# Seven-product blocks with product copies ahead of weight operations, four direct blocks for five, and attention scores on 128 rows

## The chip, the cores and the metric

The kernel runs on one core of one Trainium2 chip. TensorE (PE) multiplies, VectorE (DVE), ScalarE (ACT) and GpSimd (POOL) work on the operands, and SyncE (SP) issues nearly all transfers. The metric is the device time of one execution in microseconds (us), as the median of several runs of the same kernel.

## What is computed

Two layers, each a feed-forward network (FFN), a token mixer and a second FFN, on 512 tokens of width 1024, all in float32. The feed-forward width is 2816, or 22 blocks of 128 columns.

```python
def swiglu(h, w_in, w_out):
    gu = h @ w_in
    g, u = jnp.split(gu, 2, axis=-1)
    return (jax.nn.silu(g) * u) @ w_out

def reference(x, norm_gain, ...):
    for layer in range(DEPTH):                      # 2
        g = norm_gain[layer]
        h = swiglu(rms_norm(x, g[0]), ffn_w_in[layer, 0], ffn_w_out[layer, 0])
        x = x + 0.5 * rms_norm(h, g[1])
        h = token_mixer(rms_norm(x, g[2]), ...)
        x = x + rms_norm(h, g[3])
        h = swiglu(rms_norm(x, g[4]), ffn_w_in[layer, 1], ffn_w_out[layer, 1])
        x = x + 0.5 * rms_norm(h, g[5])
    return x
```

The mixer projects its input once and runs two groups of heads on the result: 8 attention heads of width 64 with a windowed mask, and 4 mLSTM heads of width 128 in both directions. Both groups go through one output projection.

## The kernel before

**Products.** Every float32 operand is split into two halves, `hi` (a cast on ACT) and `lo` (the difference, on DVE), and a product is the sum of three matmuls: hi by hi, hi by lo, lo by hi (lines 246 to 248 in the FFN's first product). One product of the kind used there is 4 such triples, 12 matmuls of 256 columns.

**The FFN's first product** (`ffn_in`) goes over the 22 blocks f of 128 columns of gate and up weights. The first `ne` = 5 blocks are *direct* (`block`): for each half of the tokens, the gate and the up weights are loaded, split, and multiplied in 4 products, 8 products or 96 matmuls for a whole block. The other 17 go through a Strassen-Winograd scheme (`seven`): 7 products, 84 matmuls, from sums of the weight quarters (`ws`, made on DVE at lines 311 to 314), the raw gate weights, the last quarter of the up weights (`a22`) and sums of the token quarters (`tq`, `xf`, made once at the start of the FFN). A block `seven(f, w, nxt)` also prepares the weights of the block after it, `nxt`: `nxt.sums`, `nxt.raw`, `nxt.one`, `nxt.two` and `nxt.last` each start with a cast on ACT (line 288) and go on with a difference on DVE (line 290). Between them stand the block's own evacuations of products: ACT copies `ha` and `hb` (lines 341, 352, 356), DVE sums `ht`, `hc`, `hb` (343, 362, 366). Inside `tc.manual_schedule` PE, DVE and ACT run in the order in which the code is written, so that an evacuation written behind a weight operation waits for it. Everywhere else a scheduler orders the work by its place in the program and by when buffers come free.

**Slots.** Large buffers are slots with one tile each at a time. `xf`, two tiles with sums of token quarters, lies in slots 17 and 19. At the end of the direct blocks `xx.finish()` splits `xf[0]` into `xh` and `xl` (ACT line 219, DVE line 220); after that slot 17 is free. `Weights(f)` loads the gate weights into a ring of three buffers, `raw`, and the up weights into `wu`, slot 17 + 2·(f mod 2). For f = `ne` + 1 the up weights go into the ring instead. With `ne` = 5 the first `Weights` uses slot 19.

**The mixer.** `proj_nat` projects for 128 or 256 tokens at a time. For the first four column groups the second weight half's `lo` is made on POOL (`sub=G`), while DVE still works on the norm of the sublayer's input (`post`, `pre`). `mixer_gates` makes the gates' rows with a chain of small DVE operations. `stack_pair(hp)` turns the keys and queries of a pair of attention heads: `kst` and `qsh` have 128 rows, hi and lo halves of 64 rows on top of each other, and `qsl` holds the lo half of the queries in 64 rows of one head each. `scores(n)` makes a tile of scores by two matmuls of 512 columns, `qsh` by `kst` on 128 rows (line 854) and `qsl` by `kst` on 64 rows (line 855), 64 times in the two layers. The mLSTM heads run beside the projections of the attention's operands, the attention beside the output projection, both paced in a fixed ratio.

**The start.** `pre(t, ...)` norms token tile t: two squares on ACT, a root, two products `nt` on DVE (line 178), and eight transposes on PE (line 182).

Of the kernel before, what the change touches and what calls it, by code (L numbers as in the profile page):

```python
# [41 lines left out]
def trunk_kernel(ctx, tc, x, norm_gain, ffn_w_in, ffn_w_out, mix_w_in, conv_w, conv_b,  # L42
# [58 lines left out]
    def split_w(load, n, k4, sub=None, pieces=1):  # L101
        raw = raw_tile()
        hi = wp.tile([P, 1056], F32R, tag="hi", name="hi", bufs=3)
        lo = wp.tile([P, 1056], F32R, tag="lo", name="lo", bufs=3)
        m = n * k4

        def view(w):
            return w[:, :m].rearrange("p (k c) -> p k c", k=k4)
        step = k4 // pieces
        for k in range(0, k4, step):  # L110
            r, h, l = [view(w)[:, k: k + step] for w in (raw, hi, lo)]
            load(r, k)
            A.copy(h, r)  # L113
            (sub or V).tensor_tensor(l, r, h.bitcast(F32), ALU.subtract)  # L114
        return view(hi), view(lo)
# [43 lines left out]
    def post(t, banks, y):  # L159
# [7 lines left out]
        for n in range(2):  # L167
            c = slice(n * 512, (n + 1) * 512)
            V.scalar_tensor_tensor(xs[:, t, c], y[:, c], r, xs[:, t, c], ALU.mult, ALU.add)

    def pre(t, xn, xx, ps_of):
        ss = small("pre_ss", 2)
        for n in range(2):
            A.activation(junk, xs[:, t, n * 512: n * 512 + 512], AF.Square, accum_out=ss[:, n: n + 1])
        r = rsqrt_sum((ss[:, 0:1], ss[:, 1:2]), D, EPS, "i")
        for hf in range(2):
            c = slice(hf * 512, hf * 512 + 512)
            V.scalar_tensor_tensor(xn[:, c], xs[:, t, c], r, gpre[:, c], ALU.mult, ALU.mult)
            ps = ps_of("tr")
# [72 lines left out]
    def ffn_in(layer, j, xx, late=None):  # L252
# [19 lines left out]

        def block(f, c, pieces=1):
            h = h_of(f) if hts[f] is None else hts[f]
            banks = []
            for gu in range(2):
                lo_k, hi_k = halves_of(load(f, gu, pieces, True)[:, :1024], 1024)
# [55 lines left out]
        def seven(f, w, nxt):  # L333
# [18 lines left out]
            A.copy(u2, a)  # L352
            product(c, w1, xx.t[1], True)
            if nxt:
                nxt.one()
            A.copy(s5, c)  # L356
            if nxt:
                nxt.last()
                nxt.one_ = next(nxt.one_)
            w3, w4 = w.two_  # L360
            product(a, w3, xx.t[3], False)
            V.tensor_tensor(u1, s5, a, ALU.add)
            if nxt:
                nxt.last_ = next(nxt.last_)
            product(c, w4, xx.b22, False)
# [9 lines left out]

        ne = 5
        for f in range(ne):
            block(f, left, 2 if late and f == 0 else 1)
            if late and f < 2:
                late[f]()  # L380
# [95 lines left out]

    def proj_nat(layer, xx, col, n, evac, tiles=range(NT), ps_of=None, sub=None, per=1):
        xh, xl = xx.h, xx.l
        w = mix_w_in[layer].rearrange("(k p) c -> p k c", p=P)
        parts = []  # L480
        for q in range(2):
            def load(dst, _, q=q):
                nc.sync.dma_start(dst, w[:, q * 4: q * 4 + 4, col: col + n])
            parts.append(split_w(load, n, 4, sub if q else None))
        for t0 in tiles[::per]:
# [36 lines left out]
    def mixer(layer, xx):  # L522
# [86 lines left out]
        def stack_pair(hp):  # L609
            base = (20, 4)[hp % 2]  # L610
            ks, qh = pair("kst", base), pair("qsh", base + 1)
            ql = t2("qsl", hp % 2, F32R)[:, :512]
            stack(kn, hp, ks, None)
            stack(qn, hp, qh, ql)
            stacks[hp] = (ks, qh, ql)

        def projections():
# [20 lines left out]
        def opening():  # L638
            for n, _ in enumerate(heads()):
                if n == 58:  # L640
                    stack_pair(0)
                if n in (60, 64):
                    next(att)
                yield
# [14 lines left out]
    def mixer_gates(gt):  # L659
# [44 lines left out]
        for d in range(1, 4):  # L704
            for i in range(4 - d):
                V.tensor_scalar(bb(bb_index(i, d)), bb(bb_index(i, d - 1)),
                                fl4[:, i + d - 1, P - 1: P], None, ALU.add)
        pn = psB("gnat")
        for q in range(18):
# [13 lines left out]
        return n1, n2, em  # L723

    ps_abc, ps_st = banks_of(0), banks_of(1, 2)

    def mlstm_head(h, qk, gates, vx, smo, o):
        hold = {}
        return mlstm_main(h, qk, gates, vx, hold), mlstm_tail(h, gates[2], smo, o, hold)
# [56 lines left out]
    def mlstm_tail(h, em, smo, o, hold):  # L786
# [7 lines left out]
        G.tensor_tensor(hv, hv, den.unsqueeze(3).to_broadcast([P, NT, 2, P]), ALU.mult)  # L794
        nt = one.tile([P, D], F32, tag="nt", name="cell", bufs=2)
        cell, junk = [nt[:, q * 512: q * 512 + 512].rearrange("p (t c) -> p t c", t=NT) for q in range(2)]
# [23 lines left out]
    def stack(src, hp, dh, dl):  # L820
# [9 lines left out]
        else:  # L830
            for e, s, o in ((0, lo, hi), (1, hi, lo)):
                A.copy(dh[s, e], ps[s])
                A.copy(dh[o, e], ps[s])
                V.tensor_tensor(dl[s], ps[s], dh[s, e].bitcast(F32), ALU.subtract)

    def attention(stack_pair, stacks, pts, av, mask, mm):
# [10 lines left out]
        def scores(n):  # L847
# [4 lines left out]
            c = slice(t * P, (t + 1) * P)  # L852
            hs = slice(e * HD, (e + 1) * HD)
# [139 lines left out]
```

## Time and profile before

| | us |
|---|---|
| median of 3 runs (lowest to highest) | 2105.77 (2105.02 to 2107.11) |
| the profiled execution | 2105.01 |
| its span in the trace | 2103.3 |
| PE busy | 2065.3 (98%) |
| PE weight loads busy | 1854.0 (88%) |
| DVE busy | 1529.3 (73%) |
| ACT busy | 1136.1 (54%) |
| POOL busy | 269.8 (13%) |

Busy time is the time in which an engine had at least one instruction under way. Matmuls overlap, one starting before the last has ended, so what a matmul costs is the distance from its start to the next one's (its *pitch*), not its printed duration. Times in the trace are counted from the start of the span. A bracket at the end of a row tells how long the engine had been idle before and which instruction ended that.

### The profile page before, as it was taken

To read this page: it belongs to the slowest core of one execution; us is meant where nothing else is said; L and a number is where in the kernel's file an instruction comes from. 1 tells how busy PE (TensorE), PEld (TensorE's weight loads), DVE (VectorE), ACT (ScalarE), POOL (GpSimd) and SP (SyncE) were. 2 spreads that over 40 slices of the span, in tenths; PEclk is the share of its full clock that TensorE was granted. 3 is DMA by queue.
4 is the path that set the end of the run, shared out by engine and by line. 5 is a ranking of instruction groups with operands and counts; after the bars stand their busy time and mean duration, and the time that the engine had idled before them with its cause. 6 is when DMAs were issued, how large, how long until landed. Compare 5 with 4: busy or idle time off the path is not lost. (4 is left out here: it accounts for less than half of the span.)

```text
span 2103.3 us, 35628 instructions
## 1 busy us (share of the span) xinstructions
PE 2065.3 (98%) x13918; PEld 1854.0 (88%) x13918; DVE 1529.3 (73%) x2594; ACT 1136.1 (54%) x2034; POOL 269.8 (13%) x338
## 2 busy tenths in 40 slices
PE   8999999999999999999999999999999999999998
PEld 7999988889976999998899998888898679999886
DVE  7788757785666888876787886667856668878665
ACT  6555555445564755555665554554455556555554
POOL 1000001434512100000010000014334121000000
PEclk9999999999999999999999999999999999999999
DMA  7533355541112653335564334654411136433364
GB/s 220 153 101 104 109 188 192 157 120 54 51 51 91 196 161 106 109 98 186 186 199 135 106 107 128 187 185 139 121 41 41 66 117 196 140 105 101 121 207 143
DMA packets 305886, 274.48 MB, mean 131 GB/s; under 512 B 8789, under 2 KB 275509, under 8 KB 305718
## 3 DMA queue, kind: packets, MB, share of 16 engines
q1 hardware_dynamic: 305718, 272.21, 43.1%
q8 instruction: 109, 1.79, 0.4%
q14 instruction: 59, 0.48, 0.1%
HBM read 270.08 MB, written 2.10 MB: 129 GB/s over the span
## 5 line engine op out<-in xcount | busy, mean ns | idle before, releaser
L114 DVE TENSOR_TENSOR lo<-raw,hi 128x1024 fp32r<-128x1024 f32 (+1 forms) x272 | 338.3, 1244 | 227.2 <-ACT hi L113 226.6
L113 ACT CAST hi<-raw 128x1024 fp32r<-128x1024 f32 (+1 forms) x280 | 294.7, 1053 | 322.5 <-PE o L411 227.0
L409 PE MATMUL o<-lo,hq 128*128 128x512 f32 x704 | 236.9, 394 | 0.8 <-DVE lo L114 0.8
L411 PE MATMUL o<-hi,hq 128*128 128x512 f32 x704 | 223.3, 394 | 0.0
L288 ACT CAST hi<-ws 128x1024 fp32r<-128x1024 f32 x136 | 143.1, 1052 | 147.3 <-issue 75.9
L408 PE MATMUL o<-hi,hq 128*128 128x512 f32 x704 | 210.6, 395 | 2.5 <-ACT hq L445 2.5
L492 PE MATMUL nat<-hi,xh 128*128 128x256 f32 (+1 forms) x640 | 186.8, 293 | 0.0
L493 PE MATMUL nat<-lo,xh 128*128 128x256 f32 (+1 forms) x640 | 182.1, 285 | 2.5 <-DVE lo L114 2.3
L290 DVE TENSOR_TENSOR lo<-ws,hi 128x1024 fp32r<-128x1024 f32 x136 | 166.2, 1222 | 22.3 <-ACT hi L288 22.3
L494 PE MATMUL nat<-hi,xl 128*128 128x256 f32 (+1 forms) x640 | 182.0, 286 | 0.0
L246 PE MATMUL gu<-xh,hi 128*128 128x256 f32 x640 | 180.1, 284 | 0.8 <-ACT xh L200 0.8
L247 PE MATMUL gu<-xl,hi 128*128 128x256 f32 x640 | 180.1, 283 | 0.8 <-DVE xl L201 0.8
L248 PE MATMUL gu<-xh,lo 128*128 128x256 f32 x640 | 179.2, 282 | 0.0
L408 PEld LDWEIGHTS o<-hi,hq 128*128 128x128 f32 x704 | 131.9, 188 | 34.0 <-ACT hq L445 3.4
L246 PE MATMUL pc<-xh,hi 128*128 128x256 f32 x544 | 160.0, 294 | 0.2 <-ACT hb L356 0.2
L409 PEld LDWEIGHTS o<-lo,hq 128*128 128x128 f32 x704 | 131.9, 188 | 31.4 <-DVE lo L114 1.1
L411 PEld LDWEIGHTS o<-hi,hq 128*128 128x128 f32 x704 | 132.2, 188 | 30.8
L247 PE MATMUL pa<-tq,hi 128*128 128x256 f32 x544 | 153.0, 281 | 0.0
L248 PE MATMUL pc<-xh,lo 128*128 128x256 f32 x544 | 152.8, 281 | 0.0
L247 PE MATMUL pc<-xl,hi 128*128 128x256 f32 x544 | 152.8, 281 | 0.0
L248 PE MATMUL pa<-tq,lo 128*128 128x256 f32 x544 | 152.7, 281 | 0.0
L246 PE MATMUL pa<-tq,hi 128*128 128x256 f32 x544 | 152.4, 280 | 0.0
(240 smaller groups left out, 5627.3 us busy)
## 6 DMA issues: line engine op xcount, KB each, us to landing
raw<-in_ffn_w_out_dram SPq DMA_DIRECT2D x176, 512.0 KB, 3.5
raw<-in_ffn_w_in_dram SPq DMA_DIRECT2D x150, 512.0 KB, 4.0
wu<-in_ffn_w_in_dram SPq DMA_DIRECT2D x64, 512.0 KB, 4.6
raw<-in_mix_w_in_dram SPq DMA_DIRECT2D x56, 512.0 KB, 3.8
raw<-in_mix_w_out_dram SPq DMA_DIRECT2D x32, 512.0 KB, 3.7
raw<-in_mix_w_in_dram SPq DMA_DIRECT2D x16, 528.0 KB, 4.3
gpost<-in_norm_gain_dram SPq DMA_DIRECT2D x6, 512.0 KB, 5.1
gpre<-in_norm_gain_dram SPq DMA_DIRECT2D x5, 512.0 KB, 3.5
```

The source lines that it names most:

```text
L113: A.copy(h, r)
L114: (sub or V).tensor_tensor(l, r, h.bitcast(F32), ALU.subtract)
L246: PE.matmul(ps, wh[:, k], xh[:, k], start=start and k == 0, stop=False, skip_group_check=True)
L247: PE.matmul(ps, wh[:, k], xl[:, k], start=False, stop=False, skip_group_check=True)
L248: PE.matmul(ps, wl[:, k], xh[:, k], start=False, stop=k == 3, skip_group_check=True)
L290: V.tensor_tensor(lo, src, fp(hi), ALU.subtract)
L408: PE.matmul(banks[t][n], a, wh[:, n], start=first, stop=False)
L409: PE.matmul(banks[t][n], a, wl[:, n], start=False, stop=False)
L411: PE.matmul(banks[t][n], b, wh[:, n], start=False, stop=end)
L492: PE.matmul(d, xh[:, k, tok], wh[:, k % 4], start=k == 0, stop=False)
L493: PE.matmul(d, xh[:, k, tok], wl[:, k % 4], start=False, stop=False)
L494: PE.matmul(d, xl[:, k, tok], wh[:, k % 4], start=False, stop=k == NK - 1)
```

## The change

1. In `seven`, the ACT copy `hb` (s5) comes ahead of the cast for `nxt.one`, and the DVE differences of `nxt.one` come behind the sum `hc` (u1).
2. `ne` goes from 5 to 4.
3. `qsl` has 128 rows, with a copy of each head's 64 rows made on ACT, and both matmuls of `scores` run over 128 rows. It lies in the ring `nt`, where the cell tiles of the mLSTM heads also lie; a head takes its tile when it is created.
4. `stack_pair` is made in two steps, keys and then queries, at scores 2 and 4, 9 and 11, 16 and 18 for 3, 13 and 17.
5. The `lo` halves that POOL made in the mixer are made on DVE.
6. `mixer_gates` is made in two steps, and the transposes of the gates are ordered behind the third projection group.
7. For the first two token tiles one of the two squares is made on DVE, and the first direct block's `lo` waits for the `nt` of tile 1.

```diff
-    def halves_of(src, n, sub=None):
+    def halves_of(src, n, after=None):
...
         A.copy(hi[:, :n], src)
-        (sub or V).tensor_tensor(lo[:, :n], src, hi[:, :n].bitcast(F32), ALU.subtract)
+        with tc.issue_after(after) if after else nullcontext():
+            V.tensor_tensor(lo[:, :n], src, hi[:, :n].bitcast(F32), ALU.subtract)
...
+        opening = len(first_nt) < 2
+        if opening:
+            V.tensor_tensor_reduce(out=xn[:, 512:1024], in0=xs[:, t, 512:1024], in1=xs[:, t, 512:1024], op0=ALU.mult,
+                                   op1=ALU.add, scale=1.0, scalar=0.0, accum_out=ss[:, 1:2])
+        for n in range(1 if opening else 2):
             A.activation(junk, xs[:, t, n * 512: n * 512 + 512], AF.Square, accum_out=ss[:, n: n + 1])
...
             product(c, w1, xx.t[1], True)
+            A.copy(s5, c)
             if nxt:
                 nxt.one()
-            A.copy(s5, c)
-            if nxt:
                 nxt.last()
-                nxt.one_ = next(nxt.one_)
             w3, w4 = w.two_
             product(a, w3, xx.t[3], False)
             V.tensor_tensor(u1, s5, a, ALU.add)
             if nxt:
+                nxt.one_ = next(nxt.one_)
                 nxt.last_ = next(nxt.last_)
...
-        ne = 5
+        ne = 4
...
-            run(proj_nat(layer, xx, *g, tiles=(0, 1), sub=G, per=1 + (n in (1, 2))))
+            run(proj_nat(layer, xx, *g, tiles=(0, 1), per=1 + (n in (1, 2))))
...
         gates = mixer_gates(gt)
+        next(gates)
         for n, g in enumerate(groups[1:]):
             run(proj_nat(layer, xx, *g, tiles=(2, 3), per=1 + (n < 2)))
+            if n == 1:
+                with tc.issue_after(last_ins(mybir.EngineType.PE)):
+                    gates = next(gates)
...
-            ks, qh = pair("kst", base), pair("qsh", base + 1)
-            ql = t2("qsl", hp % 2, F32R)[:, :512]
+            ks = pair("kst", base)
             stack(kn, hp, ks, None)
+            yield
+            qh = pair("qsh", base + 1)
+            ql = one.tile([P, D], F32R, tag="nt", name="qsl", bufs=2).rearrange("p (a s) -> p a s", a=2)
             stack(qn, hp, qh, ql)
...
                 A.copy(dh[o, e], ps[s])
-                V.tensor_tensor(dl[s], ps[s], dh[s, e].bitcast(F32), ALU.subtract)
+                V.tensor_tensor(dl[s, e], ps[s], dh[s, e].bitcast(F32), ALU.subtract)
+                A.copy(dl[o, e], dl[s, e].bitcast(F32))
...
             PE.matmul(ps, qh[:, e, c], ks[:, e], start=True, stop=False)
-            PE.matmul(ps, ql[hs, c], ks[hs, e], start=False, stop=True)
+            PE.matmul(ps, ql[:, e, c], ks[:, e], start=False, stop=True)
...
-                if n in (3, 13, 17):
-                    stack_pair((3, 13, 17).index(n) + 1)
+                if n in (2, 9, 16):
+                    made = stack_pair(1 + n // 7)
+                if n in (2, 4, 9, 11, 16, 18):
+                    next(made)
```

The order on ACT in a seven-product block, before (`ha` and `hb` are evacuations, `hi` and `a22` belong to the next block's weights):

```order
L352 COPY ha_946<-pa_949 128x256
L288 CAST hi_1014<-ws_978 128x1024
L356 COPY hb_947<-pc_951 128x256
L288 CAST a22_1018<-raw_944 128x512
L288 CAST hi_1048<-ws_979 128x1024
```

and after:

```order
L361 COPY ha_941<-pa_944 128x256
L363 COPY hb_942<-pc_946 128x256
L297 CAST hi_1010<-ws_973 128x1024
L297 CAST a22_1013<-wu_939 128x512
```

The copy `hb` has moved ahead of the cast of `ws`. On DVE in the same blocks, before:

```order
L290 TENSOR_TENSOR lo_985<-raw_942,hi_984 128x1024
L290 TENSOR_TENSOR lo_1015<-ws_978,hi_1014 128x1024
L362 TENSOR_TENSOR hc_948<-hb_947,pa_949 128x256
L290 TENSOR_TENSOR a22_1018<-raw_944,a22_1018 128x512
L366 TENSOR_TENSOR hb_947<-ha_946,pc_951 128x256
```

and after:

```order
L299 TENSOR_TENSOR lo_980<-raw_937,hi_979 128x1024
L369 TENSOR_TENSOR hc_943<-hb_942,pa_944 128x256
L299 TENSOR_TENSOR lo_1011<-ws_973,hi_1010 128x1024
L299 TENSOR_TENSOR a22_1013<-wu_939,a22_1013 128x512
L374 TENSOR_TENSOR hb_942<-ha_941,pc_946 128x256
```

The sum `hc` has moved ahead of the `lo` of `ws`. On DVE at the passage from the direct blocks to the first seven-product block, before (`xl_83` is the end of `xx.finish()`, `ws_919` and `ws_920` are that block's weight sums, `lo_926`, `lo_929` and `lo_932` its halves, and `ht` on line 343 is its own first evacuation):

```order
L311 TENSOR_TENSOR ws_919<-wu_917 128x512
...
L312 TENSOR_TENSOR ws_920<-raw_915,wu_917 128x512
L313 TENSOR_TENSOR ws_919<-ws_919,raw_915 128x512
L98 TENSOR_TENSOR lo_882<-raw_879,hi_881 128x1024
L314 TENSOR_TENSOR ws_920<-raw_915,ws_919 128x512
...
L290 TENSOR_TENSOR lo_929<-ws_919,hi_928 128x1024
L220 TENSOR_TENSOR xl_83<-xf_84,xh_82 128x4x256
L284 TENSOR_TENSOR ht_522<-gu_885,sil_910 128x256
L290 TENSOR_TENSOR lo_932<-ws_920,hi_931 128x1024
L343 TENSOR_TENSOR ht_522<-ha_946,pb_950 128x256
```

and after (`ws_788`, `ws_789`, `lo_798` and `lo_801` are the same things there):

```order
L229 TENSOR_TENSOR xl_83<-xf_84,xh_82 128x4x256
...
L352 TENSOR_TENSOR ht_815<-ha_816,pb_820 128x256
L320 TENSOR_TENSOR ws_848<-raw_813 128x512
L320 TENSOR_TENSOR ws_788<-wu_786 128x512
L321 TENSOR_TENSOR ws_789<-raw_784,wu_786 128x512
L299 TENSOR_TENSOR a22_803<-wu_786,a22_803 128x512
L322 TENSOR_TENSOR ws_788<-ws_788,raw_784 128x512
L323 TENSOR_TENSOR ws_789<-raw_784,ws_788 128x512
L299 TENSOR_TENSOR lo_798<-ws_788,hi_797 128x1024
L299 TENSOR_TENSOR lo_801<-ws_789,hi_800 128x1024
```

The sums and halves of the first block's weights have moved from ahead of `xl` to behind it. The transfers on SP at the same place, before (`wu_917` holds the first block's up weights):

```order
L263 DMA raw_653<-in_ffn_w_in_dram 128x8x128
L263 DMA wu_917<-in_ffn_w_in_dram 128x8x128
L263 DMA raw_684<-in_ffn_w_in_dram 128x8x128
...
L263 DMA raw_915<-in_ffn_w_in_dram 128x8x128
L263 DMA raw_942<-in_ffn_w_in_dram 128x8x128
```

and after (`wu_786` holds them there, in slot 17):

```order
L272 DMA raw_748<-in_ffn_w_in_dram 128x8x128
L272 DMA raw_784<-in_ffn_w_in_dram 128x8x128
L272 DMA raw_811<-in_ffn_w_in_dram 128x8x128
L272 DMA raw_813<-in_ffn_w_in_dram 128x8x128
L272 DMA wu_786<-in_ffn_w_in_dram 128x8x128
L272 DMA wu_939<-in_ffn_w_in_dram 128x8x128
L272 DMA raw_937<-in_ffn_w_in_dram 128x8x128
```

The load of the first block's up weights has moved behind the raw loads of the first two seven-product blocks.

## Rows read from the trace of the kernel before

**Rows 1.** The page: TensorE's busy time, share of the span, instructions.

```profile
PE 2065.3 (98%) x13918; PEld 1854.0 (88%) x13918; DVE 1529.3 (73%) x2594; ACT 1136.1 (54%) x2034; POOL 269.8 (13%) x338
```

**Rows 2.** One line's instructions, 40 to 70 us: durations ns, first to last start.

```profile
L246 PE MATMUL gu<-xh,hi x85: 279/282/287, 40.1 to 69.9; 128*128 128x256 f32 x85
```

**Rows 3.** Line 362's instructions in the first and the last FFN, same columns.

```profile
L362 DVE TENSOR_TENSOR hc<-hb,pa x17: 412/415/421, 86.3 to 250.4; 128x256 f32<-128x256 f32 x17
...
L362 DVE TENSOR_TENSOR hc<-hb,pa x17: 411/415/421, 1806.1 to 1969.7; 128x256 f32<-128x256 f32 x17
```

**Rows 4.** Timeline, first FFN, two seven-product blocks: start, duration, engine, line, operation [idle].

```profile
126.24 1.22 DVE L290 TENSOR_TENSOR lo<-ws,hi 128x1024 fp32r<-128x1024 f32 x1
...
127.38 0.41 DVE L362 TENSOR_TENSOR hc<-hb,pa 128x256 f32<-128x256 f32 x1
...
127.84 0.19 PEld L246 LDWEIGHTS pa<-tq,a 128*128 128x128 f32 x1 [0.15 <-DVE hc L362]
...
135.16 1.05 ACT L288 CAST hi<-ws 128x1024 fp32r<-128x1024 f32 x1 [0.97 <-PE pc L247]
...
136.11 0.37 ACT L356 COPY hb<-pc 128x256 f32<-128x256 f32 x1
...
136.53 0.39 PE L246 MATMUL pc<-xh,hi 128*128 128x256 f32 x1
```

**Rows 5.** Timeline, first FFN, from the end of the direct blocks on.

```profile
76.83 1.05 ACT L219 CAST xh<-xf 128x1024 fp32r<-128x1024 f32 x1 [0.15 <-PE gu L248]
...
77.91 1.23 DVE L220 TENSOR_TENSOR xl<-xf,xh 128x1024 fp32r<-128x1024 f32 x1 [0.26 <-ACT xh L219]
...
78.05 0.28 PE L246 MATMUL pa<-xh,hi 128*128 128x256 f32 x1
...
79.17 0.37 SPq L263 DMA_DIRECT2D wu<-in_ffn_w_in_dram  x1
...
82.11 0.68 DVE L312 TENSOR_TENSOR ws<-raw 128x512 f32<-128x512 f32 x1
82.71 0.69 DVE L313 TENSOR_TENSOR ws<-ws,raw 128x512 f32<-128x512 f32 x1
```

**Rows 6.** Transfers by line, at 79, 760 and 1087 us: count, KB, us to landing.

```profile
wu<-in_ffn_w_in_dram SPq DMA_DIRECT2D x1, 512.0 KB, 4.9
...
wu<-in_ffn_w_in_dram SPq DMA_DIRECT2D x1, 512.0 KB, 3.8
...
raw<-in_ffn_w_in_dram SPq DMA_DIRECT2D x1, 512.0 KB, 7.3
```

**Rows 7.** Busy time by stretch: length, engines' busy us (instructions), granted clock, DMA share, GB/s.

```profile
632.17:635.59 3.42, 3.42 (x17) 1.69 (x14) 0.00 (x0) 0.12 (x1) 0.69 (x1) 0.50 0.01 2
```

**Rows 8.** Timeline of PE in the attention of layer 0, and in its output projection.

```profile
600.81 0.40 PE L854 MATMUL sc<-kst,qsh 128*128 128x512 f32 x1
601.14 0.50 PE L855 MATMUL sc<-kst,qsl 64*128 64x512 f32 x1
601.58 0.44 PE L823 MATMUL stk<-idj,kn 128*128 128x128 f32 x2
...
636.02 0.39 PE L408 MATMUL o<-hi,mrg 128*128 128x512 f32 x1
636.25 0.39 PE L409 MATMUL o<-lo,mrg 128*128 128x512 f32 x1
```

**Rows 9.** Groups by line and shape: weight loads of the 64-row score matmuls, whole span.

```profile
L855 PEld LDWEIGHTS sc<-kst,qsl 64*128 64x128 f32 x64 | 11.7, 183 | 17.5 <-issue 16.3 <-DVE qsl L834 0.7
```

**Rows 10.** Timeline of PE around a pair's stacks, layer 0.

```profile
624.66 0.63 PE L870 MATMUL pt<-idj,sm 128*128 128x128 f32 x4 [1.01 <-ACT pts L875]
...
628.37 0.50 PE L854 MATMUL sc<-kst,qsh 128*128 128x512 f32 x1 [0.82 <-ACT qsh L833]
```

**Rows 11.** Timeline of PE at the mixer's first projections, and at the kernel's start.

```profile
399.04 0.66 PE L182 MATMUL tr<-idj,nt 128*128 128x128 f32 x4 [0.98 <-DVE nt L178]
...
14.99 2.38 PE L182 MATMUL tr<-idj,nt 128*128 128x128 f32 x8 [5.02 <-DVE nt L178]
```

More of the change, by code (lines that the diff above doesn't have):

```diff
@@ L97, in halves_of, with split_w @@
         A.copy(hi[:, :n], src)
-        (sub or V).tensor_tensor(lo[:, :n], src, hi[:, :n].bitcast(F32), ALU.subtract)
+        with tc.issue_after(after) if after else nullcontext():
+            V.tensor_tensor(lo[:, :n], src, hi[:, :n].bitcast(F32), ALU.subtract)
         return [[w[:, q: q + 512].rearrange("p (k c) -> p k c", k=4) for w in (hi, lo)] for q in range(0, n, 512)]
-    def split_w(load, n, k4, sub=None, pieces=1):
+    def split_w(load, n, k4, pieces=1):
         raw = raw_tile()
@@ L113, in split_w @@
             A.copy(h, r)
-            (sub or V).tensor_tensor(l, r, h.bitcast(F32), ALU.subtract)
+            V.tensor_tensor(l, r, h.bitcast(F32), ALU.subtract)
         return view(hi), view(lo)
@@ L169, in post @@
             V.scalar_tensor_tensor(xs[:, t, c], y[:, c], r, xs[:, t, c], ALU.mult, ALU.add)
+    first_nt = []
     def pre(t, xn, xx, ps_of):
         ss = small("pre_ss", 2)
-        for n in range(2):
+        opening = len(first_nt) < 2
[3 more added lines that the diff above has]
+        for n in range(1 if opening else 2):
             A.activation(junk, xs[:, t, n * 512: n * 512 + 512], AF.Square, accum_out=ss[:, n: n + 1])
@@ L178, in pre @@
             V.scalar_tensor_tensor(xn[:, c], xs[:, t, c], r, gpre[:, c], ALU.mult, ALU.mult)
+            if opening and hf:
+                first_nt.append(last_ins(mybir.EngineType.DVE))
             ps = ps_of("tr")
@@ L271, in h_of, with block @@
             return hts[f]
-        def block(f, c, pieces=1):
+        def block(f, c, pieces=1, after=None):
             h = h_of(f) if hts[f] is None else hts[f]
@@ L276, in block @@
             for gu in range(2):
-                lo_k, hi_k = halves_of(load(f, gu, pieces, True)[:, :1024], 1024)
+                lo_k, hi_k = halves_of(load(f, gu, pieces, True)[:, :1024], 1024, after)
                 ps = psA("gu")[:, c]
@@ L374, in seven @@
             V.tensor_tensor(h[:, right], u1, g1, ALU.mult)
-        ne = 5
+        ne = 4
         for f in range(ne):
-            block(f, left, 2 if late and f == 0 else 1)
+            block(f, left, 2 if late and f == 0 else 1, first_nt[-1] if late and f == 0 else None)
             if late and f < 2:
@@ L475, in mixer_proj_T, with proj_nat @@
         return qk
-    def proj_nat(layer, xx, col, n, evac, tiles=range(NT), ps_of=None, sub=None, per=1):
+    def proj_nat(layer, xx, col, n, evac, tiles=range(NT), ps_of=None, per=1):
         xh, xl = xx.h, xx.l
@@ L483, in load @@
                 nc.sync.dma_start(dst, w[:, q * 4: q * 4 + 4, col: col + n])
-            parts.append(split_w(load, n, 4, sub if q else None))
+            parts.append(split_w(load, n, 4))
         for t0 in tiles[::per]:
@@ L610, in stack_pair @@
             base = (20, 4)[hp % 2]
-            ks, qh = pair("kst", base), pair("qsh", base + 1)
-            ql = t2("qsl", hp % 2, F32R)[:, :512]
+            ks = pair("kst", base)
             stack(kn, hp, ks, None)
+            yield
+            qh = pair("qsh", base + 1)
+            ql = one.tile([P, D], F32R, tag="nt", name="qsl", bufs=2).rearrange("p (a s) -> p a s", a=2)
             stack(qn, hp, qh, ql)
             stacks[hp] = (ks, qh, ql)
+            yield
         def projections():
@@ L640, in opening @@
                 if n == 58:
-                    stack_pair(0)
+                    run(stack_pair(0))
                 if n in (60, 64):
@@ L707, in mixer_gates @@
                                 fl4[:, i + d - 1, P - 1: P], None, ALU.add)
+        yield
         pn = psB("gnat")
@@ L722, in mixer_gates @@
             A.activation(em[:, :, t, 1], n2[:, 7 - t, :], AF.Exp, scale=-1.0)
-        return n1, n2, em
+        yield n1, n2, em
     ps_abc, ps_st = banks_of(0), banks_of(1, 2)
     def mlstm_head(h, qk, gates, vx, smo, o):
-        hold = {}
+        hold = {"nt": one.tile([P, D], F32, tag="nt", name="cell", bufs=2)}
         return mlstm_main(h, qk, gates, vx, hold), mlstm_tail(h, gates[2], smo, o, hold)
@@ L794, in mlstm_tail @@
         G.tensor_tensor(hv, hv, den.unsqueeze(3).to_broadcast([P, NT, 2, P]), ALU.mult)
-        nt = one.tile([P, D], F32, tag="nt", name="cell", bufs=2)
+        nt = hold["nt"]
         cell, junk = [nt[:, q * 512: q * 512 + 512].rearrange("p (t c) -> p t c", t=NT) for q in range(2)]
```

1 line of the change is left out of this document (removed).

## The prediction

> **What bounds the kernel now.** I read the page's busy shares first. TensorE is busy for 2065.3 us, 98% of the span, and the next engine, VectorE, for 73% [rows 1]. So a change pays only where TensorE starts its next matmul sooner, or has fewer of them, and it costs where TensorE has to wait. The second view is therefore the distance between the starts of matmuls. In a stretch without waits, every third matmul (line 246) starts 85 times from 40.1 to 69.9 us [rows 2]: 29.8 / 84 / 3 = 0.1183 us for one matmul of 256 columns. The third view is the timeline at the places where that distance is longer. The seven-product blocks have two such places in each block, the attention scores one for each tile, and the passage from the direct blocks to the first seven-product block has none. That passage is what the change disturbs.
>
> **The change part by part.**
>
> *Order inside the seven-product blocks.* From one block to the next `hc` takes (250.4 − 86.3) / 16 = 10.26 us in the first FFN and (1969.7 − 1806.1) / 16 = 10.23 in the last [rows 3]. 84 matmuls at 0.1183 are 9.94. So 0.32 and 0.29 us are lost in a block, 0.30 on average. The timeline shows on what. DVE's `hc` starts at 127.38, behind a `lo<-ws` of 1.22 us, and the product that needs its bank starts at 127.84 after waiting for it; ACT's `hb` starts at 136.11, behind a cast of 1.05 us, and product `pc` starts at 136.53, 0.05 us after the copy's end [rows 4]. The change turns both pairs around, so each evacuation starts when its product is done. What is now late is the weight operation, by one evacuation: 0.37 us on ACT, 0.41 on DVE [rows 4]. Its product is in the next block, some 9 us off, and the DVE work of a block, four sums, three `lo`, `a22` and five evacuations, leaves about 1.3 us of a block free when I step through it with the durations of rows 4 and 5. So nothing takes the place of the two waits: 68 blocks × 0.30 = **−20.4**. If one of the two came back, −10.
>
> *Four direct blocks for five.* A direct block is 96 matmuls, a seven-product block 84: 12 × 0.1183 × 4 FFNs = **−5.7**. The weight operations of the block that moves are about the same in number, and they lie beside TensorE in both forms.
>
> *The first seven-product block.* This is the price of the step to four, and the diff shows it only through the slot number. The first `Weights` now has f = 4, so its up weights go to slot 17, which is `xf[0]`'s until `finish` has made `xl`. Before, with f = 5, they went to slot 19 and were there long before. The load now waits for DVE, and its sums and halves stand behind it. I count from F, the start of the cast `xh<-xf`, 76.83 in the first FFN. TensorE starts the first seven-product matmul at F + 1.22 (78.05) [rows 5], has two products that need only the gate weights, 24 matmuls or 2.84 us, and wants the third at F + 4.06. The operand of that one comes so:
> - `xl<-xf` ends at 77.91 + 1.23, and the next transfer to slot 17 is issued 0.03 later, at 79.17 = F + 2.34 [rows 5]. It is a load of the same kind, waiting for the same thing.
> - It lands after 3.8 to 4.9 us at this place [rows 6]; I take 4.4: F + 6.75.
> - DVE makes s1, s3, the `lo` of `a22` and s2, four operations at distances of 0.60 us with 0.69 for the last [rows 5]: F + 9.25.
> - ACT casts the sum, 1.05 [rows 4]: F + 10.3. This is when the third product may start.
> - DVE makes the `lo`, 1.22 [rows 4]: F + 11.55. The third matmul of the product wants that at F + 4.06 + 2 × 0.12 = F + 4.30.
>
> So TensorE stands for about 11.55 − 4.30 = 7.3 us. What comes next is not late again: the second block's raw weights are already there, its weight sums have the whole of the first block's last five products (60 matmuls, 7.1 us), and the load for the block after is issued when `wu` is read, some 10 us before it is used.
>
> A stop of this length costs TensorE its clock too. Around the stacks it waits 1.01 us and 0.82 us within some 4 us [rows 10], and soon after the granted clock is 0.50 for 3.42 us with TensorE busy throughout [rows 7], that is 1.2 GHz for 2.4: half of that stretch, 1.7 us, is lost. I take 1.8 behind a longer stop. 7.3 + 1.8 = 9.1, times four FFNs: **+36.4**. The ends: a landing after 3.8 us and no loss of clock, 6.7 (+27); a landing after 4.9 and twice the loss of clock, 11.4 (+46).
>
> *Scores on 128 rows.* In the attention the first score matmul starts at 600.81, the second, on 64 rows, at 601.14, and the next instruction at 601.58 [rows 8]: 0.33 + 0.44 us. A matmul of 512 columns on 128 rows takes 0.23 in the output projection (636.02 to 636.25) [rows 8]. So the pair costs 0.77 for 0.46. The weight loads of the 64-row matmuls idle 16.3 us in sum over 64 pairs before they start, with nothing that the profile shows to wait for [rows 9]. Two matmuls on 128 rows should cost 0.46, so a pair gains 0.29 (median over all 64; the rows give 0.31): 64 × 0.29 = **−18.4**. The ACT copies that fill the other 64 rows, 16 of about 0.6 us, fall where ACT has room; behind a stack they add their time to a wait that is there already. The ends: only the part before the second matmul, 64 × (0.33 − 0.23) = −6.4, and all of it with what scatters, −21.
>
> The Trainium skill, page "TensorEngine Tiling (Array Packing)", section "Tiling Modes", says that changing the tiling mode drains TensorE; rows 8 and 9 agree with 0.10 us before the 64-row matmul and 0.21 behind its start. The Trainium skill's page "TensorE: Matmul & The Clock Gate", section "Why this matters for your kernels", says that a matmul on fewer rows takes the same time as one on 128. By that sentence alone the copies would buy nothing, and the sum would be 18.4 higher; the 0.44 for 0.23 speaks against it.
>
> *Stacks in two steps.* TensorE waits 1.01 us for `pts`, which ACT makes behind a stack, and 0.82 for `qsh` [rows 10], in both layers, and then has the half-clock stretch above. Apart, keys and queries queue less on ACT. The first wait should go, the second stay. I take 1.5 for a layer: **−3**. The ends: −7 (both go, and the clock holds) and +3 (the extra copies lengthen the second).
>
> *The rest.* The `lo` halves that go from POOL to DVE free DVE's norm operations of a neighbour, and put more work on DVE just where TensorE waits 0.98 us for its `nt` [rows 11]: **−0.5**, ends ±2. The gates come in the same order on TensorE and on DVE as before: 0. At the start one square goes to DVE, which can do it while it waits for the second token tile; TensorE's wait of 5.02 us for `nt` [rows 11] is set by the landing of that tile and a chain behind it: **−0.5**, ends −1.5 and +1.
>
> **Sum:** −20.4 − 5.7 + 36.4 − 18.4 − 3 − 0.5 − 0.5 = **−12.1**. The profiled execution took 2105.01 for a span of 2103.3; it is 0.8 under the median of the three runs. From the median 2105.8 the forecast is 2093.7, say **2094**.
>
> **The rivals.**
> - *The passage costs less.* If the load were covered, or the clock stayed up, the stop would be 4 to 6.7 us in an FFN: −48.5 + 16 to 27, 2073 to 2084. For it: the loads of 3.8 us. Against it: the load cannot be issued before `xl`, and the chain behind it is six operations, each with its row. 0.13.
> - *The scores gain nothing.* If the 64-row matmul's time were that of the switch to its neighbours alone, and stayed with the transposes and `po` next to it, or if ACT's softmax chain took over, the sum is −12.1 + 18.4 = +6.3: 2112. (It is also what the Trainium skill's sentence on fewer rows would give.) Against it: the idle weight loads in rows 9, one for each pair. 0.09.
> - *The seven-product blocks stay at 10.24.* The change would then not do what it says: the weight operation that is late is waited for in the next block, −12.1 + 20.4 = +8.3: 2114. Against it: DVE's spare 1.3 us. 0.06.
> - *Slower through the landing in the open.* The one load that TensorE waits for takes what the slowest loads of this size take, 7.3 us [rows 6], for 4.4: the stop is 2.9 longer, and with a stretch at half clock twice as long as that of rows 7 the passage costs 7.3 + 2.9 + 3.4 = 13.6. −48.5 + 54.4 = +5.9: 2112. It decides from 48.5 / 4 = 12.1 us for an FFN. For it: two transfers more are queued near it. Against it: three loads at this very place took under 5. 0.12.
>
> **How the numbers follow.** The forecast, 2084 to 2104, has 0.60, its upper tenth beyond the bound of "same". What a measurement of this kernel can tell from no change is about 0.2%, 4.2 us. Faster is the forecast without that tenth (0.54) and the first rival (0.13), and a little from half-lost gains: 0.69. Same, 2101.6 to 2110: the rest of the forecast and the halves of the rivals: 0.13. Slower: 0.18. The range goes from 2072, the first rival with most of its stop gone, to 2112, where three rivals begin.
>
> **What would show each step.** A distance of 9.94 to 9.97 us from `hc` to `hc` shows the first step right; 10.2 shows it wrong. At each passage TensorE should stand some 7 us between the second and the third product, with a transfer `wu` in flight and a stretch at clock 0.50 behind it; if these are missing, the time is near 2060. The two score matmuls should start 0.23 us apart, and so should the next instruction. The prediction is wrong if the stop is under 5 or over 12 us, or if the distances in the scores stay above 0.3.

## The result, and the profile after

The changed kernel takes 2122.1 us (median of 4 runs, 2116.7 to 2123.2) for 2105.6 before; the ratio is 1.0072, with a 95% interval of 1.0054 to 1.0090. It is slower by 16.5 us. 2094 was forecast, with a range that ended at 2112.

The page of the changed kernel, first the busy times, and then the first groups of PE's waits (line and operand that waited, the instruction waited for; total us, times, longest):

```profile
PE 2041.7 (96%) x13870; PEld 1861.2 (88%) x13870; DVE 1544.4 (73%) x2634; ACT 1154.5 (54%) x2058; POOL 253.6 (12%) x330
```

```profile
PE pa L255 <- ACT hi L297: 22.3, 4, 5.7
PE tr L191 <- DVE nt L185: 12.4, 6, 4.3
PE gu L256 <- DVE xl L210: 6.6, 2, 3.6
PE gnat L727 <- DVE gates L721: 5.3, 4, 1.6
PE sc L870 <- ACT qsh L849: 3.9, 4, 1.3
```

TensorE is still the engine with the most work, but 96% of the span and not 98% [rows 1]. Its first wait is the forecast one: `pa`, the third product of the first seven-product block, four times. The third line was forecast by nothing: twice 3 to 4 us for `xl`, in the middle of the direct blocks. The second line was 9.2 us in four waits before; among its six there is now one of 3.9 us at 1090.6 us, also there.

To see where the time went I took the starts of the same matmuls in both traces and summed the differences by stage, against what the prediction's own terms give for that stage:

| stage | matmuls | forecast, us | measured, us | miss |
|---|---|---|---|---|
| start, up to the first `gu` | same | −0.5 | +0.3 | +0.8 |
| direct blocks, 4 FFNs | 384 fewer | −45.4 | −26.9 | **+18.5** |
| seven-product blocks and FFN output, 4 FFNs | 336 more | +55.7 | +55.9 | +0.2 |
| mixer up to the first scores, 2 layers | same | −0.5 | +5.4 | +5.9 |
| scores to the next FFN, 2 layers | same | −21.4 | −17.8 | +3.6 |
| sum | | −12.1 | +16.9 | +29.0 |

In the direct blocks a block of 96 matmuls at 0.1183 us (11.36 us) is gone from each FFN. The stage became shorter by 10.8, 5.0, 7.2 and 4.0.

**The order in the seven-product blocks.** The rows of the evacuation `hc` in the first and the last FFN (line 369, which answers to [rows 3]; first to last start):

```profile
L369 DVE TENSOR_TENSOR hc<-hb,pa x18: 420/422/422, 83.4 to 253.0; 128x256 f32<-128x256 f32 x18
...
L369 DVE TENSOR_TENSOR hc<-hb,pa x18: 420/422/422, 1816.7 to 1986.9; 128x256 f32<-128x256 f32 x18
```

(253.0 − 83.4) / 17 = 9.98 us and (1986.9 − 1816.7) / 17 = 10.01 for a block; it was 10.26 and 10.23. Each average has one longer distance in it, 10.84 and 10.87 us to the last block, among whose matmuls six of the FFN's output stand. The other distances are 9.92 to 9.96.

**The passage.** The timeline of the changed kernel in the first FFN (start, duration, engine, line, operation, in brackets the idle time before), DVE, SP and ACT first, and PE behind:

```profile
67.39 1.23 DVE L229 TENSOR_TENSOR xl<-xf,xh 128x1024 fp32r<-128x1024 f32 x1 [3.14 <-ACT xh L228]
...
68.64 5.97 SPq L272 DMA_DIRECT2D wu<-in_ffn_w_in_dram  x2
...
72.32 0.69 DVE L320 TENSOR_TENSOR ws<-wu 128x512 f32<-128x512 f32 x1 [0.68 <-DMA wu<-in_ffn_w_in_dram]
...
74.14 0.68 DVE L322 TENSOR_TENSOR ws<-ws,raw 128x512 f32<-128x512 f32 x1
...
74.85 1.99 ACT L297 CAST hi<-ws 128x1024 fp32r<-128x1024 f32 x2 [1.91 <-DVE ws L322]
...
75.95 0.58 PE L255 MATMUL pa<-tq,hi 128*128 128x256 f32 x1 [5.44 <-ACT hi L297]
...
77.21 0.58 PE L257 MATMUL pa<-tq,lo 128*128 128x256 f32 x1 [0.47 <-DVE lo L299]
```

The chain runs link by link as forecast: `xl` ends at 68.62, the load is issued at 68.64, lands at about 72.3 (3.7 us), and the sums, the cast and the `lo` follow. PE's starts are 5.6 and 0.8 us late. The stretches of the same place (length, then busy us and instructions of PE, PEld, DVE, ACT and POOL, granted clock, DMA share, GB/s):

```profile
67.50:70.40 2.90, 2.90 (x26) 2.80 (x24) 1.45 (x2) 0.37 (x1) 0.00 (x0) 1.00 0.16 46
70.40:75.90 5.50, 0.11 (x1) 0.00 (x0) 4.21 (x7) 1.67 (x3) 0.00 (x0) 0.87 0.29 85
75.90:81.40 5.50, 4.99 (x22) 4.69 (x23) 5.39 (x6) 2.58 (x4) 0.00 (x0) 0.51 0.63 180
81.40:84.00 2.60, 2.60 (x25) 2.60 (x24) 0.57 (x2) 1.84 (x3) 0.00 (x0) 1.00 0.52 152
```

TensorE does one matmul in 5.5 us, then the granted clock is 0.51 (1.2 GHz for 2.4) for 5.5 us: 22 matmuls where 42 would have fitted in 5 us of work. The stop was a little shorter than forecast and the slow stretch longer.

**The wait that was not forecast.** The start of the second FFN of layer 0, DVE and then PE, first in the kernel before:

```profile
723.10 1.41 DVE L178 SCALAR_TENSOR_TENSOR nt<-xs,rs_yi,gpre 128x512 f32<-128x512 f32 x2
...
729.43 1.28 DVE L201 TENSOR_TENSOR xl<-tr,xh 128x512 fp32r<-128x512 f32 x2
...
725.83 0.60 PE L182 MATMUL tr<-idj,nt 128*128 128x128 f32 x4
726.18 0.36 PE L246 MATMUL gu<-xh,hi 128*128 128x256 f32 x1
```

and in the changed kernel:

```profile
719.42 1.41 DVE L185 SCALAR_TENSOR_TENSOR nt<-xs,rs_yi,gpre 128x512 f32<-128x512 f32 x2
720.74 1.22 DVE L99 TENSOR_TENSOR lo<-raw,hi 128x1024 fp32r<-128x1024 f32 x1
...
725.15 1.28 DVE L210 TENSOR_TENSOR xl<-tr,xh 128x512 fp32r<-128x512 f32 x2
...
720.22 1.32 PE L191 MATMUL tr<-idj,nt 128*128 128x128 f32 x8
722.25 0.62 PE L255 MATMUL gu<-xh,hi 128*128 128x256 f32 x3 [0.71 <-ACT xh L209]
725.89 0.39 PE L256 MATMUL gu<-xl,hi 128*128 128x256 f32 x1 [3.01 <-DVE xl L210]
```

The direct blocks do the left half of the tokens (tiles 0 and 1) first, in all of them, and then the right half. While TensorE works on the left half, DVE norms and splits tiles 2 and 3. Counted from the first `gu` of the FFN (696.39 here, 700.12 before), DVE starts the last tile's `nt` at 23.0 us in both kernels, and its last two `xl` at 28.8 now and 29.3 before. The chain has not become slower. But TensorE has left-half work for four blocks, 4 × 48 × 0.1183 = 22.7 us, and not for five, 28.4. Before, `xl` came as TensorE ran out; now TensorE stands 0.7 us for `xh` and 3.0 us for `xl`, and the clock falls behind that. PE's row for 2 us there (length, busy us and instructions of PE, granted clock, DMA share, GB/s):

```profile
726.00:728.00 2.00, 2.00 (x11) 0.60 0.73 208
```

So it goes in the last three FFNs: the new waits are 3.7, 3.9 and 3.6 us, where 1.4 stood in sum before, and the stretches at half clock with them cost about 6.8 us in sum. Together that is 16.6 of the stage's 18.5 us.

**The scores.** PE in the attention of layer 0, which answers to [rows 8]:

```profile
574.09 0.40 PE L870 MATMUL sc<-kst,qsh 128*128 128x512 f32 x1
574.33 0.39 PE L871 MATMUL sc<-kst,qsl 128*128 128x512 f32 x1
574.56 0.28 PE L500 MATMUL nat<-hi,xh 128*128 128x256 f32 x1
```

0.24 and 0.23 us for 0.33 and 0.44. The matmul behind the pair gains as well. In the kernel before, with a `nat` behind the pair:

```profile
570.53 0.50 PE L855 MATMUL sc<-kst,qsl 64*128 64x512 f32 x1
570.96 0.39 PE L492 MATMUL nat<-hi,xh 128*128 128x256 f32 x1
571.18 0.28 PE L493 MATMUL nat<-lo,xh 128*128 128x256 f32 x1
```

and in the changed kernel the row that follows the three above:

```profile
574.67 0.28 PE L501 MATMUL nat<-lo,xh 128*128 128x256 f32 x1
```

That first `nat` has 0.22 us up to the next start behind a 64-row matmul, and 0.11 behind one on 128 rows. The weight loads of the second matmul idle for 2.4 us in the whole span where they idled for 17.5 [rows 9], of which 16.3 had no releaser that the profile shows.

### The profile page after: what moved, and what is told of

Its sections match the earlier page's. It is cut to its first block, busy times and chain, and to the rows that moved or that the text cites. A ratio compares the mean times of both kernels' runs of the same rounds, so it can differ in the third digit from the quotient of the medians.

```text
span 2120.1 us, 35561 instructions
## 1 busy us (share of the span) xinstructions
PE 2041.7 (96%) x13870; PEld 1861.2 (88%) x13870; DVE 1544.4 (73%) x2634; ACT 1154.5 (54%) x2058; POOL 253.6 (12%) x330
## 5 line engine op out<-in xcount | busy, mean ns | idle before, releaser
L115 DVE TENSOR_TENSOR lo<-raw,hi 128x1024 fp32r<-128x1024 f32 (+1 forms) x280 | 348.8, 1246 | 241.4 <-ACT hi L114 241.3
L297 ACT CAST hi<-ws 128x1024 fp32r<-128x1024 f32 x144 | 151.2, 1052 | 70.9 <-ACT a L297 62.1
L255 PE MATMUL pa<-tq,hi 128*128 128x256 f32 x576 | 164.6, 286 | 22.3 <-ACT hi L297 22.3
L299 DVE TENSOR_TENSOR lo<-ws,hi 128x1024 fp32r<-128x1024 f32 x144 | 175.2, 1219 | 1.5 <-ACT hi L297 1.5
L257 PE MATMUL pa<-tq,lo 128*128 128x256 f32 x576 | 165.0, 286 | 1.9 <-DVE lo L299 1.9
L256 PE MATMUL pa<-tq,hi 128*128 128x256 f32 x576 | 164.8, 286 | 0.0
L257 PE MATMUL pc<-xh,lo 128*128 128x256 f32 x576 | 163.4, 284 | 0.0
L256 PE MATMUL pc<-xl,hi 128*128 128x256 f32 x576 | 163.4, 284 | 0.0
L256 PE MATMUL gu<-xl,hi 128*128 128x256 f32 x512 | 147.4, 289 | 6.6 <-DVE xl L210 6.6
L255 PE MATMUL gu<-xh,hi 128*128 128x256 f32 x512 | 146.8, 290 | 4.6 <-ACT xf L236 3.7
L257 PE MATMUL gu<-xh,lo 128*128 128x256 f32 x512 | 146.3, 288 | 0.0
```

Source lines behind the costliest of these rows:

```text
L115: V.tensor_tensor(l, r, h.bitcast(F32), ALU.subtract)
L255: PE.matmul(ps, wh[:, k], xh[:, k], start=start and k == 0, stop=False, skip_group_check=True)
L256: PE.matmul(ps, wh[:, k], xl[:, k], start=False, stop=False, skip_group_check=True)
L257: PE.matmul(ps, wl[:, k], xh[:, k], start=False, stop=k == 3, skip_group_check=True)
L299: V.tensor_tensor(lo, src, fp(hi), ALU.subtract)
```

## The experiments

**Five direct blocks again.** The changed kernel with one number put back.

```diff
-        ne = 4
+        ne = 5
```

> The changed kernel with five direct blocks for four, all else as changed. Theory (the loss comes from the step to four): its trace shows 7.9 to 9.4 us more than 18 clean blocks at each passage from the direct blocks to the first seven-product block, 35 us in sum, and 18.5 us of waits and half clock inside the direct blocks, against 5.7 us of matmuls saved. With five: 2122.1 - 35 - 18.5 + 5.7 = 2074 us, and no wait of TensorE over 1 us in the direct blocks. Rival (the waits inside the direct blocks come from another part, such as the ring nt that qsl now shares with the norm's tiles): only the passage goes, 2122.1 - 35 + 5.7 = 2093 us, with waits of 3 to 4 us left at the starts of the FFNs.

2069.4 us (2068.8 to 2071.4), ratio 0.983 to before (0.981 to 0.984). So the kernel with four direct blocks is 52.7 us slower than this one, and without that step the rest of the change gains 36 us. It is also 4.6 us under the expected 2074. In the traces 5.8 of the 52.7 us lie from the scores to the next FFN, which the edit doesn't touch: there the clock stayed at 1.00 in this trace and fell in that of the changed kernel. The waits inside the direct blocks are gone in the FFNs that follow a mixer (the stage is 58.7 and 58.5 us as before); in the second layer's first FFN the two waits of 0.6 and 0.8 us that stand there before stay. The rival, by which another part brings these waits, falls. PE at the same place as above (the FFN's first `gu` is at 686.45), with no bracket on any row:

```profile
712.16 0.60 PE L191 MATMUL tr<-idj,nt 128*128 128x128 f32 x4
712.52 0.36 PE L255 MATMUL gu<-xh,hi 128*128 128x256 f32 x1
...
712.84 0.60 PE L191 MATMUL tr<-idj,nt 128*128 128x128 f32 x4
```

The transposes of the last tile go between matmuls of the fifth block's left half.

**Four direct blocks with the early load.** The slot is counted from the first seven-product block, so that its up weights go to slot 19.

```diff
-            raw = chunk("wu", 17 + 2 * (f % 2)) if gu and not whole_f else raw_tile()
+            raw = chunk("wu", 17 + 2 * ((f - ne + 1) % 2)) if gu and not whole_f else raw_tile()
```

> The changed kernel with four direct blocks, and the slot of the up weights counted from the first seven-product block, so that its load goes to slot 19, free early. Theory (the passage waits for the load that slot 17 holds back): the waits of 5.6 and 0.8 us in each FFN and the half clock behind them go, 35 us: 2087 us; the waits inside the direct blocks stay. Rival (the passage waits for the order on DVE and ACT, not for the load): 2120 us or more.

2085.3 us (2084.7 to 2086.8). The passage's waits are gone, and with them 36.8 us: this is the price of the load that slot 17 holds back (34.9 by the starts of matmuls in its own stages, and 2.1 from the scores to the next FFN). The rival, by which the order on DVE and ACT holds the passage up, falls. The second product and the third follow without a gap:

```profile
70.27 0.28 PE L257 MATMUL pb<-xh,lo 128*128 128x256 f32 x1
70.39 0.28 PE L255 MATMUL pa<-tq,hi 128*128 128x256 f32 x1
```

The waits of the direct blocks are still there (`gu` for `xl` 7.1 us in two waits). This kernel and the one with five differ by 15.9 us, where four blocks have 5.7 us of matmuls less: 21.6 us are missing. By the starts of matmuls 18.5 of these are lost in the direct blocks, for the cover; 3.7 lie from the scores to the next FFN, where the clock fell in this trace and not in the one with five.

**Three direct blocks.** The same, with `ne = 3`.

> The run with four direct blocks and the early load, with three direct blocks in place of four. Theory (the left-half products of the direct blocks cover the norm of the right tokens on DVE, each block 5.7 us of it, and what is not covered TensorE waits out): 5.7 us of matmuls fewer, and 5.7 us of wait more in at least the last three FFNs, 2085.3 - 5.7 + 17 to 23 = 2097 to 2102 us, with waits of 8 us and more where there were 3.6. Rival (the waits are one chain's order and not cover): 2080 us.

2090.3 us (2088.2 to 2093.0), 5.0 us more than with four, and 7 us under the 2097 that I had expected at least. The direction is that of cover: another 5.7 us of matmuls are gone and the time goes up by 5, so that the rival (2080) falls. The size is not, and the waits are 5.7 to 7.1 us, not 8 and more. PE and DVE at the start of layer 0's second FFN (first `gu` at 688.42):

```profile
712.14 1.97 PE L191 MATMUL tr<-idj,nt 128*128 128x128 f32 x8 [5.67 <-DVE nt L185]
715.21 0.58 PE L256 MATMUL gu<-xl,hi 128*128 128x256 f32 x1 [0.27 <-DVE xl L210]
...
714.47 0.69 DVE L210 TENSOR_TENSOR xl<-tr,xh 128x512 fp32r<-128x512 f32 x1
...
715.67 0.69 DVE L210 TENSOR_TENSOR xl<-tr,xh 128x512 fp32r<-128x512 f32 x1
```

`nt` starts at the same 22.9 us, and now it is what TensorE waits for. But the last `xl` start at 26.1 and 27.3, not at 28.7: a direct block also puts two `lo` of 1.2 us on DVE, and with a block less these no longer stand ahead of `xl`. A direct block is cover for TensorE and load for DVE; I had counted the first only.

**The order in the seven-product blocks alone**, in the kernel before (the diff is the part of the change at `product(c, w1, xx.t[1], True)`).

> The kernel before with the new order inside the seven-product blocks alone. Theory: from hc to hc 9.96 us for 10.24, 68 blocks, 2105.6 - 19 = 2086.6 us. Rival (with five direct blocks the order brings new waits in the next block): less than half of that, over 2096 us.

2088.6 us (2087.0 to 2089.0): −17.0. The four stages with these blocks are shorter by 4.9, 4.7, 5.0 and 4.2, together 18.7; the trace is longer by some 2 us in other stages that the edit doesn't touch.

**The scores on 128 rows alone**, in the kernel before, with the stacks in one step at the old places. As in the change, a head takes its cell tile when it is created; these two lines are not shown.

```diff
-            ql = t2("qsl", hp % 2, F32R)[:, :512]
+            ql = one.tile([P, D], F32R, tag="nt", name="qsl", bufs=2).rearrange("p (a s) -> p a s", a=2)
...
-                V.tensor_tensor(dl[s], ps[s], dh[s, e].bitcast(F32), ALU.subtract)
+                V.tensor_tensor(dl[s, e], ps[s], dh[s, e].bitcast(F32), ALU.subtract)
+                A.copy(dl[o, e], dl[s, e].bitcast(F32))
...
-            PE.matmul(ps, ql[hs, c], ks[hs, e], start=False, stop=True)
+            PE.matmul(ps, ql[:, e, c], ks[:, e], start=False, stop=True)
```

> The kernel before with the scores on 128 rows alone; stacks in one step at the old places. Theory: the pair of score matmuls 0.46 us for 0.77, 64 times, 2105.6 - 18 = 2087.6 us. Rival (the extra copies on ACT lengthen the stacks' waits): each of six stacks later by 1.2 us and the half clock longer, 2096 us.

2079.7 us (2078.7 to 2080.9): −25.9, 8 more than expected. The two stages with scores are shorter by 5.6 and 7.9 in layer 0, and 5.5 and 6.4 in layer 1. Most of this is in the matmuls. A pair gains 0.29 us (median over 64), 18.4 us in sum, as expected; the matmul behind the pair starts its successor 0.06 to 0.11 us sooner, about 5 us over 54 of the 64 pairs, and that had not been expected. The waits do not gain: TensorE's idle time (gaps above 0.15 us) from the scores to the next FFN is 2.5 us in each layer before, and 2.5 and 2.4 here. In layer 0 another 1.7 us is clock, which fell behind the stacks before [rows 7] and does not here. In layer 1 it had not fallen before either, behind the same waits of 1.0 and 0.8 us. First layer 1 in the kernel before (PE alone), then layer 0 in this run:

```profile
1672.00:1674.00 2.00, 2.00 (x14) 1.00 0.00 0
```

```profile
627.00:632.00 5.00, 5.00 (x32) 3.41 (x31) 2.95 (x7) 3.10 (x5) 0.10 (x1) 1.00 0.00 0
```

**Order and scores together**, and nothing else of the change: the two edits above in the kernel before.

> The kernel before with the new order in the seven-product blocks and the scores on 128 rows, and nothing else of the change. Theory (the two gains are in different stages and add): 2105.6 - 17.0 - 25.9 = 2062.7 us, below the changed kernel with five direct blocks by 6.7. Rival (the parts left out, stacks in two steps, gates, opening, DVE for POOL, carry a share of that kernel's gain): 2070 us or more.

2062.2 us (2060.9 to 2063.4), ratio 0.979 (0.978 to 0.981). The gains add, and this is the fastest kernel of the study, 43 us under the one before and 60 under the changed one. The parts that it leaves out bring nothing together: the changed kernel with five direct blocks has them all and is 7 us slower, so the rival falls.

**With the stacks in two steps** on top of that.

```diff
-            ks, qh = pair("kst", base), pair("qsh", base + 1)
+            ks = pair("kst", base)
             stack(kn, hp, ks, None)
+            yield
+            qh = pair("qsh", base + 1)
...
-                if n in (3, 13, 17):
-                    stack_pair((3, 13, 17).index(n) + 1)
+                if n in (2, 9, 16):
+                    made = stack_pair(1 + n // 7)
+                if n in (2, 4, 9, 11, 16, 18):
+                    next(made)
```

> The run with the new order and the scores on 128 rows, and the stacks in two steps as changed. Theory (the steps only spread the stacks' waits, and lose some: in the run with five direct blocks they are 1.4, 0.6 and 1.0 us in a layer for 1.1 and 1.0 in the run of the scores alone, and the stage from the output projection to the next FFN is 0.6 and 1.1 us longer): 2 us slower, 2064.7. Rival (the steps shorten the waits): 2061 us or less.

2069.6 us (2069.2 to 2070.7): 7.4 us slower, more than the 2 expected. PE around the stacks of layer 0, first with one step:

```profile
614.77 0.63 PE L869 MATMUL pt<-idj,sm 128*128 128x128 f32 x4 [0.96 <-ACT pts L874]
...
618.61 0.74 PE L853 MATMUL sc<-kst,qsh 128*128 128x512 f32 x2 [0.69 <-ACT qsh L832]
```

and with two:

```profile
613.15 0.66 PE L872 MATMUL pt<-idj,sm 128*128 128x128 f32 x4 [0.52 <-POOL sm L865]
...
616.89 0.50 PE L856 MATMUL sc<-kst,qsh 128*128 128x512 f32 x1 [1.26 <-ACT qsh L835]
...
618.26 0.50 PE L857 MATMUL sc<-kst,qsl 128*128 128x512 f32 x1 [0.43 <-ACT qsl L837]
619.46 1.22 PE L856 MATMUL sc<-kst,qsh 128*128 128x512 f32 x2 [0.70 <-ACT qsh L835]
```

The wait for `pts` is gone, as forecast. The wait for `qsh` is longer, since the queries made behind score 18 are those that score 20 wants, and the copy that fills `qsl` is now waited for by itself. From the scores to the next FFN TensorE is idle for 0.8 and 1.0 us more in the two layers. With the waits the clock falls to 0.50 in both layers, and about 3.4 us are lost to it each time; the same stretch in layer 0 with one step and with two:

```profile
620.00:624.00 4.00, 4.00 (x26) 2.81 (x26) 1.20 (x3) 1.34 (x3) 0.69 (x1) 1.00 0.01 4
```

```profile
620.00:624.00 4.00, 4.00 (x17) 2.45 (x17) 1.19 (x3) 1.34 (x4) 0.69 (x1) 0.50 0.02 4
```

**POOL back in the mixer**, in the changed kernel with five direct blocks (the `sub=G` of the kernel before).

> The changed kernel with five direct blocks, and the second weight half of the mixer's first projections split on POOL again. Theory (DVE has more to do where TensorE waits for its norm, and the mixer's first two stages are longer by 1.0 and 1.6, 0.8 and 1.6 us for that): 2069.4 - 4.9 = 2064.5 us. Rival (those stages are longer for another reason, such as the order of the gates): 2069 us.

2068.5 us (2067.6 to 2069.1) for 2069.4 without: hardly less, where 4.9 was expected. The time is the rival's (2069), but not for the rival's reason: in the stage itself the theory holds. Up to the first `projT` and up to the first `gnat` the trace is shorter by 0.8, 1.5, 0.7 and 1.6 us, and these stages are back at the lengths of the kernel before. But the same trace is 2.6 and 2.2 us longer from the scores to the next FFN, which the edit doesn't touch: there the clock fell in this run and held in the other, and TensorE waits 0.6 to 0.8 us more in each layer for a `sm` of POOL. The same 4 us of dense work behind the stacks, with five direct blocks and then with POOL back:

```profile
622.60:626.60 4.00, 4.00 (x28) 2.64 (x28) 1.65 (x4) 1.76 (x5) 0.69 (x1) 1.00 0.02 4
```

```profile
620.30:624.30 4.00, 4.00 (x23) 2.42 (x21) 1.15 (x3) 1.31 (x3) 0.69 (x1) 0.61 0.01 4
```

So 4.6 us are shown in the stage's matmul starts, and hardly 1 in the time. Why the clock held in the one trace and fell in the other, with the same waits ahead of it (1.26, 0.43 and 0.70 us in both), stays open. It is not a matter of the kernel alone: of the four executions with five direct blocks two have a mean granted clock of 0.998 (2068.8 and 2068.9 us; the profiled one is of these) and two have 0.994 (2069.9 and 2071.4 us).

The gates and the start have no run of their own. The run with POOL back differs from the stacks in two steps by these two parts alone, and is 1.1 us faster, little more than the spread of one kernel's times.

## Why the prediction was wrong

**The step that failed** is that of the four direct blocks, the term of −5.7. The prediction counts their matmuls, and of the rest it says that the weight operations "lie beside TensorE in both forms". It asked what work the block adds and what hides that, and not what the block itself hides. Its left-half product is the last thing that TensorE can do while DVE norms tiles 2 and 3. In place of −5.7 the step costs +15.9 without the passage, or +12.8 by the starts of matmuls in the direct blocks: there 18.5 us were lost that the prediction put at nothing. Comparing the four- and five-block kernels shows it, and three blocks bound it: with a further block less, only 10.7 us more are lost (5.0 + 5.7), since DVE is relieved too. With the loss in it the sum would have been 6 to 10 us over the kernel before and not 12 under it. It could have been seen beforehand: in the kernel before, the transposes of the last tile start 25.7 us behind the first `gu`, among matmuls of the fifth block's left half, and in the second layer's first FFN two waits of 0.6 and 0.8 us already stand behind it. None of the signs that the prediction gave for being wrong came up, since all of them look at the passage and the scores.

**The passage**, +36.4, was right: 36.8 by the run with the early load, 34.9 in its own stages. The path and the wait came as forecast. That the size agrees so well is in part luck: inside the term two errors cancel, a stop of 6.4 us for 7.3 (the load landed after 3.7 us) and a slow stretch of 5.5 us for 3.6.

**The order of the seven-product blocks**, −20.4: 9.92 to 9.96 us from block to block, as forecast; −17.0 alone, and 18.7 in its own stages.

**The scores**, −18.4: 0.47 us for a pair as forecast. −25.9 alone, because the prediction counts the pair and not the matmul behind it (about 5 us), and because one stretch of half clock was gone (1.7 us). The rival by which they gain nothing fell. The Trainium skill's page "TensorE: Matmul & The Clock Gate", section "Why this matters for your kernels", has its sentence on fewer rows of a single matmul on 32 rows; these runs show that it does not carry over to matmuls of 64 rows among others of 128. What the Trainium skill's page "TensorEngine Tiling (Array Packing)", section "Tiling Modes", says of a drain agrees with the runs: without the change of mode the idle time before the second matmul's weight loads is 2.4 us for 17.5.

**The stacks**, −3: the sign was wrong. The steps cost 7.4 us, most of it clock (about 3.4 us in each layer of that trace). "The first wait should go, the second stay" was right of the first and wrong of the second, which grew and was joined by one for `qsl`. The half clock that the prediction sees behind the waits of both layers is in layer 0 alone in the trace before.

**The mixer**, −0.5 with ends of ±2: +5.4 in the stage. DVE could not take POOL's `lo` for nothing. In the changed kernel TensorE waits 1.6 us for `nt`, then 0.5, then 0.9 for `xl` at the first `projT`, where one wait of 0.98 stood [rows 11]. The cost of the stage is shown by the run with POOL back; of the net time only 0.9 is shown.

**The start**, −0.5: the first `gu` comes at 17.0 to 18.4 us in the traces with the old form and at 17.6 to 18.5 with the new, so nothing can be said. **The gates**: their waits stayed at 5.3 us, as forecast.

**The slower rival** that was given, a load landing after 7.3 us, did not happen. The kernel became slower by a mechanism that was not on the list. By the medians the parts sum to the whole: order and scores −43.4, stacks +7.4, gates and start −1.1, DVE for POOL +0.9, direct blocks +15.9 and passage +36.8 make +16.5.

## What to carry to other kernels

Before work is taken from the bound engine, ask what that work covers: find the chain that ends as it ends, and how much is to spare. Where buffers go round by an index, changing the index's start changes who waits for whom; a shift of one put a load behind the last reader of its slot, and a shift back was worth 35 to 37 us. And judge parts of a change one by one: here two parts gained 43 us and the others lost 60.

## What the runs showed of the hardware

A matmul on 64 rows between matmuls on 128 cost 0.44 us up to the next start, and with the start before it 0.77 us for the pair, against 0.47 on 128 rows throughout. The 128-row matmul behind it cost more too: 0.22 us for 0.12 with 256 columns, 0.34 for 0.23 with 512 (medians over 22 and 10 places). Filling the unused rows by copies on another engine was worth about 23 us over 64 pairs, 18 in the pairs and 5 behind them.

With four waits that sum to 2.9 us within 7 us, none above 1.3 us, TensorE's granted clock fell to 0.50 in the traces of the changed kernel, of the stacks in two steps and of POOL back, and held at 1.00 in the trace with five direct blocks. In the kernel before it fell in layer 0 and held in layer 1, behind the same waits of 1.0 and 0.8 us. Such a fall cost 1.7 to 3.4 us. A stage can differ by that much between kernels, layers and executions that have the same instructions in it, so a difference of that size is read from matmul starts in the edited stage and not from the whole time.
